# Encoder layer on one core: ten of 22 inner tiles by seven products in the first down stage, and another order of first norm, attention scores and tail

## The chip, the cores and the metric

The kernel runs on one core of a Trainium2 chip. The metric is the device time in microseconds of one execution. The kernel before has a median of 1548.7 us over 3 runs (1548.59 to 1549.08).

## The reference

One step of an encoder layer over 576 tokens (512 of a new stream, 64 of a running one), width 1024, inner width of the FFN 2816, which is 22 tiles of 128:

```
h = LN1(ALPHA * x + 0.5 * swiglu_ffn(x, w_gu, w_down))
z = h @ w_in          # mLSTM q, k, v, o, i, f | attention q, k, v | gates g_m, g_a
h = LN2(ALPHA * h + w_out(sig(g_m) * P_m(mLSTM(h)) + sig(g_a) * P_a(BandAttn(h))))
y = LN3(ALPHA * h + 0.5 * swiglu_ffn(h, w_gu2, w_down2))

swiglu_ffn(x, w_gu, w_down) = (silu(gate) * up) @ w_down     # gate, up = split(x @ w_gu)
```

All in float32, with 4 mLSTM heads of 256 and 16 attention heads of 64, and the new states of both returned.

## The kernel before, in words

**Numbers.** Data lie transposed: a tile is 128 features by 576 tokens, taken as two halves of 288 (slices `A` and `B`). TensorE multiplies in a rounded format. So each operand is split in a rounded high part and the rest, the low part, and a product of a weight tile and a data half is three matmuls: high by high, high weight by low data, low weight by high data (L135 is the helper `mm`). For a weight piece of 128x1024, ScalarE makes the high part `wh` (L149, `act`) and VectorE subtracts to get the low part `wl` (L152, `tt`). Some low parts are made instead by ScalarE and a DMA of POOL that adds the weight from memory (`add_lo`, L195). Takes of results out of PSUM are `stt` (L155) or `tt`.

**Order of the work.** The program is written out in the order of TensorE's matmuls. Everything else is queued with `later(time, function)` and issued as a running count of TensorE time passes by; a scheduler then puts the instructions of each engine in a fixed order by priority (`hot` raises it, `issue_after` ties an instruction behind another). Each engine works through its own list in that order. Weights come through a plan: `pump` (L232) loads the next raw piece with SP into one of 2 buffers `wr`, then splits it into one of `NWB` = 4 pairs `wh`, `wl`; `take` and `done` (L296, L306) mark use and release.

**The first down stage** (`ffn`, L1203; from 256.05 us of the profile to 392.6). The output has 8 tiles of 128. Output tiles 1, 3 and 5 are half made ahead by `plain` (L1132), one matmul triple for each inner tile and token half. For a pair of output tiles (j, j+1) `seven` (L1150) covers eight of the 22 inner tiles: it treats the two outputs, two groups of four inner tiles and the two token halves as a 2x2 by 2x2 product and makes it with seven products instead of eight, on sums of weights and sums of data. Each product is 4 tiles x 3 = 12 matmuls of 288 columns, 84 for the pair. The sums of weights come in four pieces: `a` (the two blocks of output j: a11, a12), `t` (t0, t1), `u` (q1, a22) and `v` (q0). `split_ds` (L209) makes three sums of 128x512 on VectorE into the raw buffers when `t` is due, and a fourth into a buffer of its own for `v`. The products run in the order a11, a12, t0, q1, q0, t1, a22, with takes (`ln.take`) after the first and third to seventh. The remaining 14 inner tiles are `plain` in two pieces of 8 and 6 (`DC`, L375). For j = 6 the two outputs' plain parts run before the seven.

**Hidden tiles.** `Hidden.upto` (L1111) splits the hidden activations into high and low parts `h`, `hb`, `hc` in the order `ORDER`, each tied behind the one before. `Inner.part` (L866) makes the sums of data and their parts.

**First norm** (`Norm`): squares and sums `s1`, `s2` are gathered as output tiles finish (`last`, L599; `moments`, L632); `stats` makes mean and variance with matmuls on columns of ones, POOL takes the power, `spread` and `apply` (L755) multiply by gain and 1/sigma (`stt` with `rb` from PSUM), add the bias on ScalarE and split the result for the first product with `w_in`. For the tiles 0 and 1 this is done at high priority.

**Attention.** `att_qkv(j)` (L1487) prepares head pair group j, `att_core` (L1607) makes its scores: for each block a score matmul, a VectorE pass that adds the bias and takes the minimum (L1627), exp on ScalarE, reciprocal (L1619) and scaling on VectorE or POOL (L159), a transpose on TensorE. Between them run products with `w_in`. `dup` writes keys once more, rounded (`kh`) and rest (`kl`).

**Tail** (`turned`, L701): the third norm's last tile, with columns of sums and a matmul `mb` with the mean, then 8 transposes, four `stt` of 128x512 and four stores.

Of the kernel before, what the change touches and what calls it, by code (L numbers as in the profile page):

```python
# [88 lines left out]
def tile_layer(ctx: ExitStack, tc: tile.TileContext, ins, outs):  # L89
# [92 lines left out]
    HALVED = {("in", c + j) for c in (32, 40) for j in range(3, KT)}  # L182
# [26 lines left out]
    def split_ds(c):  # L209
# [3 lines left out]
        lo = wpool.tile([P, 1024], F32R, tag="wl", name=nm("wl"), bufs=NWB)  # L213
        a, b = slice(0, 512), slice(512, 1024)
# [17 lines left out]
    def pump(limit=None):  # L232
        limit = limit or wst["ahead"]
        while True:
# [9 lines left out]
            if wst["dma"] < min(len(plan), c + 2):  # L244
# [6 lines left out]
                wst["load"] = SP.dma_start(raws[i][:, :src.shape[1]], src)  # L251
# [7 lines left out]
            if c < wst["stop"] and plan[c][0][0][:2] != "ds" and c < wst["taken"] + limit and wst["used"] < NWB:  # L259
# [10 lines left out]
                else:  # L270
                    lo = wpool.tile([P, 1024], F32R, tag="wl", name=nm("wl"), bufs=NWB)
                    step = n if plan[c][0] not in PIECES else 512
                    if plan[c][0] in HALVED:
                        for a in (0, 512):
                            act(hi[:, a:a + 512], raw[:, a:a + 512])
# [99 lines left out]
    DC = ((0, 8), (8, 8), (16, 6))  # L375
# [5 lines left out]
    def plan_ffn(n):  # L381
# [5 lines left out]
        def chunk(j, c):  # L387
            k0, nk = DC[c]
# [123 lines left out]
    class Norm:  # L512
# [86 lines left out]
        def last(self, j, cc, end=None):  # L599
# [3 lines left out]
            act(sq, d, AF.Square)  # L603
            tt(s1, s1, d, ALU.add)
# [96 lines left out]
        def turned(self, hf, dh, sq):  # L701
# [11 lines left out]
            for q, s in ((0, s1), (1, self.hs(self.s2, hf)), (0, dh), (1, sq)):  # L713
# [4 lines left out]
                if q == 0:  # L718
                    mm(mb, ones_d, s, s is s1, s is dh)
# [5 lines left out]
            for q in range(2):  # L725
                for b, a in enumerate(blocks):
# [5 lines left out]
                    stt(y, pts[b, q], rs[:, b:b + 1], self.gb[2 + q], ALU.mult, ALU.add)  # L732
                    SP.dma_start(outs["yt"][b, :, q * 512:(q + 1) * 512], y)
# [21 lines left out]
        def apply(self, j, hf, rb):  # L755
# [8 lines left out]
            early = j < 2 and self.gi == 0  # L764
# [38 lines left out]
    class Combos:  # L803


        def __init__(self, xs, raw, sums, nx=NX):
            self.xs, self.raw, self.n, self.sums, self.nx = xs, raw, 0, sums, nx
            self.own = 4
            self.b = {}
# [5 lines left out]
        def begin(self, i):  # L815
            r1, r2 = self.raw[4 + i], self.raw[i]
# [5 lines left out]
        def add(self, i, begun=False):  # L822
            r1, r2 = self.raw[4 + i], self.raw[i]
# [33 lines left out]
    class Inner(Combos):  # L857


        def __init__(self, xs, raw):  # L860
            super().__init__(xs, raw, {})

        def tile(self):
            return slot(F32R)

        def part(self, i):  # L866
# [4 lines left out]
            for n, (ka, kb) in ((1, ("t2", "t4")), (0, ("t1", "t3"))):  # L871
                t, hi, lo = self.sums.pop(2 * i + n), self.tile(), self.tile()
# [5 lines left out]
        def rest(self):  # L878
            a, b = slice(0, HT_), slice(HT_, T)
            for i in range(4):  # L880
                (h1, l1), (h2, l2) = self.xs.p[12 + i], self.xs.p[8 + i]
# [220 lines left out]
    class Hidden(Act):  # L1102


        ORDER = (*range(KT), *range(2 * KT, FT), *range(12, 2 * KT), *range(KT, 12))

        def __init__(self, raw, pools):
            super().__init__([None] * FT)
            self.raw, self.pools, self.prev, self.n = raw, pools, (None, None), 0

        def upto(self, i):  # L1111
            while self.n <= min(i, FT - 1):
                i_, j = self.n, self.ORDER[self.n]
                pool, tag, n = self.pools[(i_ >= NH0) + (i_ >= NH1) + (i_ >= FT // 2)]
                hi, lo = (pool.tile([P, T], F32R, tag=tag, name=nm(tag), bufs=n) for _ in range(2))

                a, b = self.prev
                with tc.issue_after(a.ins) if i_ else nullcontext():
                    a = ACT.activation(hi, self.raw[j], AF.Copy)
                with tc.issue_after(b.ins) if i_ else nullcontext():  # L1120
                    b = tt(lo, self.raw[j], f(hi), ALU.subtract)
# [10 lines left out]
    def plain(n, ts_, hp, cs=(0, 2)):  # L1132

        for c in cs:
            k0, nk = DC[c]
# [14 lines left out]
    def seven(n, j, inner, ln, Y=None, first=None):  # L1150
# [5 lines left out]
        def product(ps, what, xk, start, end=None):  # L1156
            w_, c0 = at[what]
            for w in "atuv":
                if w_ not in ids and w not in ids:
                    ids[w] = take((f"ds{n}", j, w))  # L1160
            wh, wl = parts[ids[w_]]
            for i in range(4):
                ww = slice(c0 + i * P, c0 + (i + 1) * P)
# [16 lines left out]
        if first is None:  # L1180
# [6 lines left out]
            ln.take(j + 1, A, X, ALU.subtract)  # L1187
            return Y, Z
# [9 lines left out]
        product(Z, "t1", "b22", False, "t")  # L1198
        return Y, Z
# [3 lines left out]
    def ffn(xs, n, gi, raw, final=None, prev=None):  # L1203
        hh = {}
        with tc.tile_pool(name=nm("hr"), bufs=FT, side="right", reuse_waits="tile") as hr, \
# [47 lines left out]
            with wstack, tc.tile_pool(name=nm("st"), bufs=1, side="right", reuse_waits="tile") as un.tp, \  # L1253
                    tc.tile_pool(name=nm("sx"), bufs=1, side="right", reuse_waits="tile") as sx:
                combos.pool = un.pool = sx
                hp_ = Hidden(hh, [(h0, "h0", 2 * NH0), None, None, (hr, "h", FT + 1)])
# [30 lines left out]
            n1, n2 = 2 * (NH1 - NH0), FT - 2 * NH1  # L1287
            with tc.tile_pool(name=nm("h1"), bufs=n1, side="right", reuse_waits="tile") as h1, \
# [8 lines left out]
                inner = Inner(hp_, [hh[k] for k in range(8, 16)])  # L1297
                for i in range(4):
# [18 lines left out]
                od.force(lambda: inner.n == 4)  # L1317
# [31 lines left out]
                if n == 1:  # L1349
# [15 lines left out]
                    ln.last(7, B, False)  # L1365
# [1003 lines left out]
```

## Time and profile before

| what | us |
|---|---|
| median of 3 runs | 1548.7 |
| the profiled execution | 1548.38 |
| its span | 1546.7 |
| TensorE busy (11587 matmuls) | 1533.1 |
| VectorE, ScalarE, POOL busy | 1138.6, 898.0, 229.1 |
| first down stage | 256.05 to 392.29 |
| first matmul with w_in behind the norm | 392.63 |
| first store's issue | 1541.63 |

The profile is of one execution; times within it count from the start of its span. Views name a group by its line, engine and tiles: `mm<-s,wh` writes PSUM tile mm from data s and weight wh; `128x288` is the shape of one operation. A number in brackets behind a row is the idle time ahead of it on that engine, with the operation that ended it.

### The profile page before, as it was taken

The numbers are of one execution on the slowest core, as the hardware profiler recorded it, in microseconds if no ns is written. First come the engines' busy times: TensorE is split into PE (matmuls) and PEld (weight loads), VectorE is DVE, ScalarE is ACT, GpSimd is POOL, SyncE is SP. The second block draws the span as 40 slices with busy tenths as digits, with TensorE's granted clock in tenths as the row PEclk, the third lists the DMA queues.
The fourth block names the chain that finished last, engine by engine and source line by source line (L and its number), as shares of the span: only waits on it lengthen the run. The fifth ranks groups of instructions, "written<-read, shape, count | busy, mean of one in ns | idle before, by whom it ended". The sixth has DMA issues, their size and how long they took to land.

```text
span 1546.7 us, 29517 instructions
## 1 busy us (share of the span) xinstructions
PE 1533.1 (99%) x11587; PEld 1518.9 (98%) x11587; DVE 1138.6 (74%) x2114; ACT 898.0 (58%) x1710; POOL 229.1 (15%) x430
## 2 busy tenths in 40 slices
PE   9999999999999999999999999999999999999998
PEld 9999999999999999999999999999999999999998
DVE  7877778675869866777586766755686877788765
ACT  7545457433865667777854877753466454457333
POOL 1000000000210025655311223202111000001000
PEclk9999999999999999999999999999999999999999
DMA  9322223533664448677534755642665323226334
GB/s 261 109 105 87 98 94 91 140 103 99 195 176 141 150 137 212 161 205 175 124 131 143 185 144 139 163 144 82 195 158 128 110 82 109 83 71 147 120 113 150
DMA packets 80259, 211.15 MB, mean 137 GB/s; under 512 B 9080, under 2 KB 20984, under 8 KB 80120
## 3 DMA queue, kind: packets, MB, share of 16 engines
q1 hardware_dynamic: 65144, 169.15, 33.1%
q0 software_dynamic: 11808, 34.28, 12.8%
q10 hardware_dynamic: 3168, 5.83, 1.2%
q8 instruction: 91, 1.49, 0.4%
q14 instruction: 48, 0.39, 0.1%
HBM read 172.27 MB, written 21.63 MB: 125 GB/s over the span
## 4 chain that ended last, share of the span: by engine, by line
PE 47%; DVE 2%; ACT 2%; issue 2%; POOL 1%; POOLq 0%; DVEq 0%; ACTq 0%
PE mm L135 39%; PE aux L135 8%; PE aux L145 1%; ACT wh L149 0%; DVE U L155 0%; ACT L149 0%; DVE tx L152 0%; DVE s L155 0%; ACT sc L149 0%; ACT s L149 0%; DVE wl L152 0%; POOL kh L159 0%; ACT wh L907 0%; ACT D L149 0%; DVE kwl L155 0%
## 5 line engine op out<-in xcount | busy, mean ns | idle before, releaser
L135 PE MATMUL mm<-s,wh 128*128 128x288 f32 (+2 forms) x3659 | 751.4, 298 | 2.6 <-ACT s L149 1.7
L135 PEld LDWEIGHTS mm<-s,wh 128*128 128x128 f32 x3659 | 587.9, 189 | 6.7 <-ACT s L149 2.2
L135 PE MATMUL mm<-s,wl 128*128 128x288 f32 (+2 forms) x1802 | 532.5, 295 | 0.0
L135 PEld LDWEIGHTS mm<-s,wl 128*128 128x128 f32 x1802 | 339.8, 189 | 0.0
L149 ACT ACTIVATE wh<-wr 128x1024 fp32r<-128x1024 f32 (+2 forms) x143 | 134.3, 948 | 152.0 <-PE mm L135 85.4
L152 DVE TENSOR_TENSOR wl<-wr,wh 128x1024 fp32r<-128x1024 f32 (+2 forms) x93 | 107.9, 1168 | 50.0 <-ACT wh L149 49.9
L135 PE MATMUL mm<-tx,wh 128*128 128x288 f32 x677 | 140.5, 296 | 0.8 <-DVE tx L152 0.8
L135 PEld LDWEIGHTS mm<-tx,wh 128*128 128x128 f32 x677 | 109.2, 188 | 1.3 <-DVE tx L152 1.0
L135 PE MATMUL mm<-tx,wl 128*128 128x288 f32 x350 | 103.2, 295 | 0.0
L152 DVE TENSOR_TENSOR wl<-wt,wh 128x1024 fp32r<-128x1024 f32 x51 | 63.8, 1250 | 53.1 <-ACT wh L907 53.0
L907 ACT ACTIVATE wh<-wt 128x1024 fp32r<-128x1024 f32 x51 | 54.0, 1059 | 79.2 <-DVE wt L152 78.1
L152 DVE TENSOR_TENSOR wl<-wu,wh 128x1024 fp32r<-128x1024 f32 x63 | 77.1, 1223 | 29.3 <-ACT wh L907 29.3
L907 ACT ACTIVATE wh<-wu 128x1024 fp32r<-128x1024 f32 x63 | 66.7, 1058 | 40.9 <-PE mm L135 35.3
L135 PE MATMUL mm<-tx,ah 128*128 128x288 f32 x416 | 85.1, 296 | 0.0
L197 POOL DMA_DIRECT2D s<-s x16 | 13.7, 858 | 468.7 <-DVE hb L152 426.7
L149 ACT ACTIVATE h<-h 128x288 f32<-128x288 f32 x78 | 34.0, 436 | 60.9 <-DVE h L152 60.9
L152 DVE TENSOR_TENSOR wl<-ws,wh 128x1024 fp32r<-128x1024 f32 x51 | 62.2, 1220 | 8.9 <-ACT wh L907 8.8
L135 PEld LDWEIGHTS mm<-tx,ah 128*128 128x128 f32 x416 | 66.3, 188 | 0.5 <-ACT c L149 0.4
L135 PEld LDWEIGHTS mm<-tx,wl 128*128 128x128 f32 x350 | 65.7, 188 | 0.0
L152 DVE TENSOR_TENSOR ws<-wu 128x1024 f32<-128x1024 f32 (+1 forms) x55 | 64.7, 1176 | 0.0
L135 PE MATMUL mm<-h,wh 128*128 128x288 f32 (+2 forms) x304 | 62.6, 296 | 0.0
L135 PE MATMUL mm<-tx,al 128*128 128x288 f32 x208 | 61.1, 294 | 0.0
(406 smaller groups left out, 3492.4 us busy)
## 6 DMA issues: line engine op xcount, KB each, us to landing
wu<-in_w_gu SPq DMA_DIRECT2D x78, 512.0 KB, 4.3
wr<-in_w_in SPq DMA_DIRECT2D x48, 512.0 KB, 4.2
wr<-in_w_dn SPq DMA_DIRECT2D x37, 512.0 KB, 3.7
wl<-in_w_in POOLq DMA_DIRECT2D x36, 512.0 KB, 6.5
wu<-in_w_in SPq DMA_DIRECT2D x24, 512.0 KB, 4.7
wr<-in_w_dn SPq DMA_DIRECT2D x19, 384.0 KB, 3.2
s<-s POOLq DMA_DIRECT2D x16, 288.0 KB, 3.6
wu<-in_w_ap SPq DMA_DIRECT2D x8, 512.0 KB, 4.7
```

What stands on the lines that cost most here:

```text
L135: PE.matmul(out, lhsT, rhs, start=start, stop=stop, **kw)
L145: PE.transpose(out, in_, idn)
L149: return ACT.activation(out, in_, func, **kw)
L152: return (eng or DVE).tensor_tensor(out, a, b, op=op)
L197: return POOL.dma_start(lo, src, accum_op=ALU.add)
L907: self.last = ACT.activation(hi, src, AF.Copy)
```

## The change

1. *First down stage.* `seven` takes ten inner tiles for outputs in four pairs: five by five, so 15 matmuls a product, 105 a pair; `plain` keeps 12 inner tiles (8 and 4). The fifth blocks of both outputs come as one more piece `e`, ahead of `a`, `t`, `u`, `v`: two loads of 128x256 into one raw buffer, four sums of 128x128 on VectorE, then high and low part 128x896. `e` holds one of the four weight buffers until the seven ends. Inner tiles are now (12, 13, 14, 15, 17) with (8, 9, 10, 11, 16); the upper ones are held as 288-wide halves, and 16 is the last that is split. Its fifth sums live in buffers `h5`.
2. *First norm.* The square and sum of output 7's second half are issued 3200 later and behind the sixth centred tile; tiles 0 to 3 of the first token half (0 and 1 of the second) are applied at high priority.
3. *Attention.* The low part of the copied keys is tied behind the core's last score; roundings of past keys behind the scaling on POOL (first core) or the last score. Two pieces of `w_in` are rounded in halves.
4. *Tail.* The `mb` matmuls come behind all column sums, the last row's store in two parts.

```
-    HALVED = {("in", c + j) for c in (32, 40) for j in range(3, KT)}
+    HALVED = {("in", c + j) for c in (32, 40) for j in range(2, KT)}
...
+        if what == "e":
+            w = raws.pop(c)
+            a12, a11, t1, t0, a22, q1, q0 = (w[:, i * P:(i + 1) * P] for i in range(7))
+            tt(q0, a11, q1, ALU.add)
+            tt(q1, a22, q1, ALU.add)
+            tt(t0, q1, a11, ALU.add)
+            tt(t1, t0, a12, ALU.add)
+            act(hi[:, :7 * P], w[:, :7 * P])
+            tt(lo[:, :7 * P], w[:, :7 * P], f(hi[:, :7 * P]), ALU.subtract)
+            parts[c] = (hi, lo)
+            return
...
-    DC = ((0, 8), (8, 8), (16, 6))
+    DC = {1: ((0, 8), None, (18, 4)), 2: ((0, 8), (8, 8), (16, 6))}
+    INNER = {1: ((8, 9, 10, 11, 16), (12, 13, 14, 15, 17)), 2: ((8, 9, 10, 11), (12, 13, 14, 15))}
+    AT5 = {"a12": 0, "a11": 1, "t1": 2, "t0": 3, "a22": 4, "q1": 5, "q0": 6}
...
         def seven(j, order="uv"):
+            if n == 1:
+                plan.append(((f"ds{n}", j, "e"), tuple(ins[f"w_dn{n}"][j + e][:, 16 * P:18 * P] for e in range(2))))
             for e, x in enumerate("at"):
...
-        def last(self, j, cc, end=None):
+        def last(self, j, cc, end=None, behind=None):
...
-                if q == 0:
-                    mm(mb, ones_d, s, s is s1, s is dh)
+            for s in (s1, dh):
+                mm(mb, ones_d, s, s is s1, s is dh)
...
-                    stt(y, pts[b, q], rs[:, b:b + 1], self.gb[2 + q], ALU.mult, ALU.add)
-                    SP.dma_start(outs["yt"][b, :, q * 512:(q + 1) * 512], y)
+                    n = 256 if q and b == nb - 1 else 512
+                    for c in range(0, 512, n):
+                        stt(y[:, c:c + n], pts[b, q][:, c:c + n], rs[:, b:b + 1], self.gb[2 + q][:, c:c + n], ALU.mult, ALU.add)
+                        SP.dma_start(outs["yt"][b, :, q * 512 + c:q * 512 + c + n], y[:, c:c + n])
...
-            early = j < 2 and self.gi == 0
+            early = self.gi == 0 and j < (2 if hf else 4)
...
-            for w in "atuv":
+            for w in "eatuv"[n == 2:]:
...
-            wh, wl = parts[ids[w_]]
-            for i in range(4):
-                ww = slice(c0 + i * P, c0 + (i + 1) * P)
+            for i in range(inner.m):
+                wh, wl = parts[ids[w_ if i < 4 else "e"]]
+                ww = slice(c0 + i * P, c0 + (i + 1) * P) if i < 4 else slice(AT5[what] * P, (AT5[what] + 1) * P)
...
-                    ln.last(7, B, False)
+                    later(3200, lambda: ln.last(7, B, False, ln.centred))
...
-                    tt(l_[r, cc], src[r], f(h_[r, cc]), ALU.subtract)
+                    with tc.issue_after(cores[j - 1]["sample"].ins) if e == 0 else nullcontext():
+                        tt(l_[r, cc], src[r], f(h_[r, cc]), ALU.subtract)
...
-                with tc.issue_after(new[1].ins):
+                with tc.issue_after((cores[0]["scaled"] if j == 1 else new[1]).ins):
...
-            later(6000 + 500 * e, lambda e=e: dup(kp, T, NPAST, e))
+            later(6000 + 500 * e, lambda e=e: when("scaled" if j == 1 else "sample", lambda: dup(kp, T, NPAST, e)))
```

**First place: VectorE in the first seven (outputs 0 and 1).** In the kernel before, from the low part of `u` on: `wl_512` is `u`, `wl_518` is `v`, `s_434` and `s_435` are takes (`s_435` from `mm_514` is that of product 1), `h_510` is the low part of the last hidden tile of product 2.

```order
L152 TENSOR_TENSOR wl_501_3361<-wr_470_3218,wh_500_3360 128x1024
L152 TENSOR_TENSOR wl_512_3434<-wr_473_3224,wh_511_3433 128x1024
L155 SCALAR_TENSOR_TENSOR s_434_3040<-s_434_3040,aux_496_3348 128x288
L155 SCALAR_TENSOR_TENSOR s_434_3040<-s_434_3040,aux_497_3349 128x288
L152 TENSOR_TENSOR wl_518_3478<-h_502_3362,wh_517_3477 128x512
L152 TENSOR_TENSOR h_510_3418<-h_241_1624,h_509_3417 128x576
L155 SCALAR_TENSOR_TENSOR s_435_3042<-s_435_3042,mm_514_3471 128x288
```

The same place in the changed kernel, on VectorE: `wr` rows are sums of `t`, `wl_514` is `t`, `wl_524` is `u`, `wl_527` is `v`, `h_519` is the low part of hidden tile 16, and `s_435` from `mm_520` is the take of product 1 and then of product 3.

```order
L155 SCALAR_TENSOR_TENSOR s_434_3040<-s_434_3040,aux_493_3318 128x288
L152 TENSOR_TENSOR wr_496_3333<-wr_496_3333 128x512
L152 TENSOR_TENSOR wr_473_3225<-wr_496_3333,wr_473_3225 128x512
L155 SCALAR_TENSOR_TENSOR s_435_3042<-s_435_3042,mm_520_3456 128x288
L152 TENSOR_TENSOR wr_473_3225<-wr_473_3225 128x512
L152 TENSOR_TENSOR wl_514_3420<-wr_473_3225,wh_513_3419 128x1024
L152 TENSOR_TENSOR wl_524_3463<-wr_496_3333,wh_523_3462 128x1024
L152 TENSOR_TENSOR wl_527_3500<-h_515_3421,wh_526_3499 128x512
L152 TENSOR_TENSOR h_519_3445<-h_321_2239,h_518_3444 128x576
L155 SCALAR_TENSOR_TENSOR s_435_3042<-s_435_3042,mm_520_3456 128x288
```

The take of product 1 stood behind all of t, u, v and the last hidden part; now it stands ahead of the last sum of t, the low parts of t, u and v, and `h_519`.

**Second place: VectorE in the third seven (outputs 4 and 5).** In the changed kernel `s_536` from `mm_580` is the take of product 1, the `wr` rows are the three sums of `t`, `wl_576` is its low part.

```order
L152 TENSOR_TENSOR s2_431_3035<-s2_431_3035,sq_579_3973 128x288
L155 SCALAR_TENSOR_TENSOR s_536_3596<-s_536_3596,mm_580_3978 128x288
L152 TENSOR_TENSOR wr_572_3886<-wr_572_3886 128x512
L152 TENSOR_TENSOR wr_567_3847<-wr_572_3886,wr_567_3847 128x512
L152 TENSOR_TENSOR wr_567_3847<-wr_567_3847 128x512
L152 TENSOR_TENSOR wl_576_3941<-wr_567_3847,wh_575_3940 128x1024
L152 TENSOR_TENSOR wl_584_3985<-wr_572_3886,wh_583_3984 128x1024
```

All sums of `t` stand behind the take.

**Third place: VectorE behind the statistics of the first norm.** In the changed kernel `s_537` from `mm_623` is the take of the last half tile of the down stage, `wl_652` and `wl_661` are the low parts of the second and third pieces of `w_in` (in halves of 512), `s_657` and `s_659` are low parts of normed tiles.

```order
L152 TENSOR_TENSOR s_657_4588<-s_535_3594,s_656_4587 128x288
L152 TENSOR_TENSOR s_537_3598<-s_537_3598,mm_623_4370 128x288
L152 TENSOR_TENSOR s_659_4603<-s_433_3038,s_658_4602 128x288
L152 TENSOR_TENSOR s1_430_3034<-s1_430_3034,s_537_3598 128x288
L152 TENSOR_TENSOR s2_431_3035<-s2_431_3035,sq_667_4645 128x288
L152 TENSOR_TENSOR wl_652_4564<-wr_644_4530,wh_651_4563 128x512 x2
L152 TENSOR_TENSOR s_537_3598<-s_537_3598,c0_429_3033 128x288
L152 TENSOR_TENSOR s_538_3600<-s_538_3600,c0_429_3033 128x288
L155 SCALAR_TENSOR_TENSOR s_536_3596<-s_536_3596,cols_129,aux_645_4541 128x288
L155 SCALAR_TENSOR_TENSOR s_434_3040<-s_434_3040,cols_129,aux_645_4541 128x288
L152 TENSOR_TENSOR sel_4657<-ident_133 64x4
L152 TENSOR_TENSOR wl_661_4614<-wr_650_4561,wh_660_4613 128x512 x2
```

In the kernel before, the low parts of the first two pieces and of half the third stood ahead of that take; now the second stands behind the take and its sums, and the third behind two more tiles of centring and two of gain.

More of the change, by code (lines that the diff above doesn't have):

```diff
@@ L808, in __init__ @@
             self.own = 4
+            self.m = len(raw) // 2
             self.b = {}
@@ L871, in part @@
             for n, (ka, kb) in ((1, ("t2", "t4")), (0, ("t1", "t3"))):
-                t, hi, lo = self.sums.pop(2 * i + n), self.tile(), self.tile()
+                t = self.sums.pop(2 * i + n)
+                hi, lo = ((slot(F32R) if i < 4 else slot(F32R, self.more, "h5", bufs=4)) for _ in range(2))
                 act(hi, t)
@@ L1102, in tile_layer, with __init__ @@
     class Hidden(Act):
-        ORDER = (*range(KT), *range(2 * KT, FT), *range(12, 2 * KT), *range(KT, 12))
-        def __init__(self, raw, pools):
+        def __init__(self, raw, pools, inner):
             super().__init__([None] * FT)
             self.raw, self.pools, self.prev, self.n = raw, pools, (None, None), 0
+            second, first = inner
+            self.ORDER = (*(k for k in range(FT) if k not in first + second), *first, *second)
+            self.half = first if len(first) > 4 else ()
         def upto(self, i):
@@ L1198, in seven @@
         product(Z, "t1", "b22", False, "t")
+        done(ids["e"])
         return Y, Z
@@ L1605, in att_qkv @@
         return st
+    cores = []
     def att_core(j, st):
+        cores.append(st)
         ap_ = apool[0]
```

75 lines of the change are left out of this document (48 added, 27 removed).

## Prediction

> **What bounds the kernel now.** I read the page first, then the chain of waits, the list of who waited for whom, the windows around the first layer norm, and last the timelines of the places that the change touches.
>
> ```profile
> span 1546.7 us, 29517 instructions
> PE 1533.1 (99%) x11587; PEld 1518.9 (98%) x11587; DVE 1138.6 (74%) x2114; ACT 898.0 (58%) x1710; POOL 229.1 (15%) x430
> 1208.90 189.75 PE mm L135 x1428
> ```
>
> TensorE is busy 1533.1 of 1546.7 us; nothing else comes near. The third row is one stretch of the chain: 1428 matmuls of 288 columns in 189.75 us, or 0.133 us each. So a matmul taken out is worth 0.133 us, and every wait that TensorE is made to keep adds its own length. What TensorE waits for now is little:
>
> ```profile
> PE mm L135 <- ACT s L149: 1.7, 1, 1.7
> PE aux L145 <- POOL sc L159: 1.2, 2, 1.0
> 399.27 0.88 PE L135 MATMUL mm<-s,wh 128*128 128x256 f32 x2 [1.73 <-ACT s L149]
> ```
>
> The columns of the first two are total, times, longest. The largest is one gap of 1.73 us, in the first product with w_in just behind the first norm. It has a tail, seen in the windows (granted clock is the number after POOL's):
>
> ```profile
> core 0: us, PE busy (x) PEld busy (x) DVE busy (x) ACT busy (x) POOL busy (x), PEclk, DMA share, GB/s
> 256.00:300.00 44.00, 44.00 (x335) 44.00 (x334) 33.30 (x55) 26.20 (x39) 5.17 (x6) 1.00 0.53 128
> 300.00:386.00 86.00, 86.00 (x650) 85.70 (x650) 58.62 (x97) 28.52 (x48) 1.02 (x2) 1.00 0.35 108
> 401.40:404.70 3.30, 3.30 (x15) 3.01 (x14) 3.30 (x10) 3.30 (x7) 0.00 (x0) 0.50 0.20 70
> 404.80:480.00 75.20, 75.20 (x563) 75.17 (x563) 58.57 (x93) 51.62 (x92) 10.01 (x14) 1.00 0.62 166
> ```
>
> From 256 to 386, the whole down stage of the first FFN, TensorE never rests. After the gap it ran 15 matmuls in 3.30 us at clock 0.50; at the rate of the last row (75.20/563 = 0.134 us) they take 2.0. One such spell costs 1.3 us.
>
> **The change part by part.** *Fewer matmuls.* A pair of output tiles took 84 matmuls by seven products and twice 84 plain; now it takes 105 and twice 72, three fewer. Four pairs: 12 x 0.133 = **-1.6 us**. Sure, if nothing waits.
>
> *What the seven products wait for.* The durations:
>
> ```profile
> L155 DVE SCALAR_TENSOR_TENSOR c<-c,mm 128x288 f32<-128x288 f32 x10 | 4.5, 447 | 0.0
> L152 DVE TENSOR_TENSOR wr<-wr 128x512 f32<-128x512 f32 x8 | 5.5, 692 | 0.2
> L149 ACT ACTIVATE wh<-wr 128x1024 fp32r<-128x1024 f32 x21 | 22.0, 1058 | 36.2 <-DVE wr L152 16.8 <-PE aux L135 10.0 <-PE mm L135 9.4
> L152 DVE TENSOR_TENSOR wl<-wr,wh 128x1024 fp32r<-128x1024 f32 x21 | 25.5, 1224 | 16.6 <-ACT wh L149 16.6
> L152 DVE TENSOR_TENSOR wl<-h,wh 128x512 fp32r<-128x512 f32 x4 | 2.8, 691 | 0.3
> L149 ACT ACTIVATE wh<-h 128x512 fp32r<-128x512 f32 x4 | 2.5, 632 | 13.1 <-PE mm L135 9.4 <-PE aux L135 3.7
> L152 DVE TENSOR_TENSOR h<-h,h 128x576 fp32r<-128x576 f32 x11 | 8.3, 754 | 0.1
> 289.18 0.85 DVE L155 SCALAR_TENSOR_TENSOR s<-s,aux 128x288 f32<-128x288 f32 x2 [2.18 <-PE aux L135]
> 290.11 0.69 DVE L152 TENSOR_TENSOR wl<-h,wh 128x512 fp32r<-128x512 f32 x1
> 290.83 0.76 DVE L152 TENSOR_TENSOR h<-h,h 128x576 fp32r<-128x576 f32 x1
> ```
>
> The last three rows are VectorE in the first seven of before: two takes, the low part of v, and the low part of the last hidden tile, done at 291.6. TensorE needs that one in the fourth tile of product 2, 21 matmuls after the seven began at 289.4, at 292.2: 0.6 us to spare. Now the order is another (the first place shown with the change). The take of product 1 waits for its 15th matmul; call its end T. Behind it on VectorE stand the last sum of t, the low parts of t, u and v, and only then the low part of hidden tile 16, which TensorE wants as fifth tile of product 2, 13 matmuls or 1.73 us after T. VectorE gets there at T + 0.45 (take) + 0.69 (sum) + 1.06 (ScalarE rounds t) + 1.22 (t) + 1.2 (u) + 0.69 (v) + 0.75 = 6.06, 6.1 with the handoffs. TensorE waits 6.1 - 1.73 = **4.35 us**. Were t, u and v ready all along, it would still be ScalarE's 0.63 for v (v's buffer comes free one tile earlier) + 0.69 + 0.75 = 2.1 behind the fourth tile, less 3 matmuls: the floor is about 1.7.
>
> *Third seven (tiles 4, 5).* All three sums of t stand behind the take of product 1: 0.45 + 3 x 0.69 + 1.06 = 3.6 us after T the rounded t is there, and product 3 wants it after 15 matmuls, at 2.0: 1.65 lost with handoffs; its low part comes 1.25 later, when two matmuls (0.27) have run: 1.0 more. **2.7 us**, floor 0 if the takes came sooner. *Second seven.* The shift of tile 0 (two matmuls on a copy) waits for takes that stand behind the sums of t, whose load waits for the new piece e. I find 0 to 2 us, take **0.5**, since the row of this wait in before shows nothing. *Fourth:* the sums have 72 plain matmuls' time; nothing.
>
> *First norm.* In before:
>
> ```profile
> 386.95 0.46 DVE L152 TENSOR_TENSOR s<-s,sq 128x288 f32<-128x288 f32 x1 [0.85 <-ACT sq L149]
> 387.32 1.93 DVE L152 TENSOR_TENSOR s<-s,c 128x288 f32<-128x288 f32 x5
> 389.17 1.29 DVE L152 TENSOR_TENSOR wl<-wr,wh 128x512 fp32r<-128x512 f32 x2
> 390.74 0.93 DVE L155 SCALAR_TENSOR_TENSOR s<-s,cols,aux 128x288 f32<-128x288 f32 x2
> L149 ACT ACTIVATE s<-s,cols 128x288 f32<-128x288 f32 x5 | 2.4, 524 | 0.0
> 392.63 0.38 PE L135 MATMUL mm<-s,wh 128*128 128x256 f32 x1
> 393.43 0.38 PE L135 MATMUL mm<-s,wh 128*128 128x256 f32 x1 [0.42 <-DVE s L152]
> ```
>
> Back to back, a subtraction costs 0.37 (1.93 for five, the last 0.45), a gain 0.42, a half low part 0.60. Now four tiles of the first half are applied at once instead of two. That removes the 1.73 us wait, but the low parts of w_in pieces fall behind (the third place shown with the change). On before's clock the chain starts at 386.95: sum 0.37, four subtractions 1.48, four gains 1.7, s1 0.37, then low parts of tile and weight 0.37 + 0.60 + 0.37 + 0.60, with ScalarE (two operations of about 0.5 for each of four tiles, and a piece's two of 0.63 between) holding the next one to about 393.4; then the take of the last tile, 0.45, a low part 0.65, s1, s2 0.8 and the second piece's half 0.69: 396.1. TensorE starts w_in at 392.25, runs five matmuls of 256 columns (0.133 x 256/288 = 0.118) and waits from 393.0: 3.1. Three matmuls on, the third piece's low part stands behind 0.60 + 2 x 0.37 + 2 x 0.42 + 0.15 + 0.65 = 3.0, less 0.36: 2.6. In sum 5.7 and 0.25 for a piece's rounding, against 3.0 + 0.4 lost in before (0.2, 0.7, 0.2, 1.9 and 0.4 over the usual spacing) and 0.4 from the earlier start: **+2.2**, from -3.4 (all waits and the slow spell gone) to +3.5.
>
> *The clock.* A wait of 1.73 us was followed by a slow spell. New waits over that: first seven, third seven; the norm has one as before. 2 x 1.3 = **+2.6**, from 0 to 5.2 (two spells for 4.35 us, one for the second seven, a second at the norm).
>
> *Attention.*
>
> ```profile
> 612.98 1.25 DVE L152 TENSOR_TENSOR kl<-s,kh 64x576 fp32r<-64x576 f32 x1
> 614.26 0.48 DVE L1627 CUSTOM_DVE_ANT_0 sc<-aux,G 64x320 f32<-64x320 f32 x1
> 614.90 0.30 PE L145 MATMUL aux<-ident,sc 128*128 128x128 f32 x1 [0.69 <-DVE mx L1627]
> 659.66 1.24 DVE L152 TENSOR_TENSOR kl<-s,kh 64x576 fp32r<-64x576 f32 x1
> 661.48 0.39 PE L135 MATMUL aux<-kh,qs 128*128 128x256 f32 x1 [0.59 <-DVE mx L1627]
> 594.87 0.40 POOL L159 TENSOR_SCALAR kl<-kl 64x256 fp32r<-64x256 f32 x1
> 595.37 0.59 POOL L159 TENSOR_SCALAR sc<-sc,mx 128x384 f32<-128x384 f32 x1
> 596.01 0.33 PE L145 MATMUL aux<-ident,sc 128*128 128x128 f32 x1 [0.96 <-POOL sc L159]
> ```
>
> The first two gaps come of a 1.25 us subtraction ahead of the last score; the change moves it behind, and 1.25 exceeds both gaps, so both go (0.69 + 0.59). At 595.37 the scaling stood behind six roundings of past keys; now it is ahead of them: 0.96 more. What is late next: the keys moved back, which TensorE needs a core later (the same subtraction comes again 46.7 us on). The halved pieces cost ScalarE 0.2 us more each beside 42% idle time. **-2.3**, from -3 to +1 (keys late once by a rounding and a subtraction on POOL).
>
> *Tail.* rsqrt's inputs come first, mean's last:
>
> ```profile
> 1539.36 0.17 ACT L149 ACTIVATE m<-aux 128x2 f32<-128x2 f32 x1
> 1540.12 0.70 POOL L509 TENSOR_TENSOR rs<-var,mhalf 128x2 f32<-128x2 f32 x1 [16.66 <-DVE var L155]
> 1540.85 1.41 DVE L155 SCALAR_TENSOR_TENSOR s<-aux,rs,s 128x512 f32<-128x512 f32 x2 [0.82 <-POOL rs L509]
> ```
>
> The four mean matmuls (256 columns, 0.5 us in all) now follow the sums instead of standing among them, and the two engines take the variance before the mean's two operations; so rs is ready 0.5 to 1 us earlier, but the mean then ends about where rs does now, and the first output row gains little; the split of the last one saves part of a 0.7 us operation and adds a store's issue. **-0.2**, from -0.6 to +0.3.
>
> Sum: -1.6 + 4.35 + 2.7 + 0.5 + 2.2 + 2.6 - 2.3 - 0.2 = +8.25. On the profiled execution (1548.38, span 1546.7 and 1.7 around it) that is 1556.6; the median of the runs, 1548.7, lies 0.3 above. I take **1556.5**.
>
> The skill has a rule here. "TensorE: Matmul & The Clock Gate", Part 1 (The HAM clock gate), of the Trainium skill has the half rate set in after at least one idle window of about 3.4 us, windows running freely. The trace agrees on the length of the spell (clock 0.50 in 401.40 to 404.70) but not on the cause: the 1.73 us wait was enough. By the page alone only the wait of 4.35 us could lower the clock.
>
> **The rivals.**
>
> *A, faster: the waits are not there.* Low parts come in time wherever they stand, as they do in before from 256 to 386, and the norm's gap and its spell go too. Then -1.6 - 3.4 - 1.3 - 2.3 - 0.2: 1539.6. It decides if hidden tile 16's low part ends within 1.73 us of T; the sum above would have to be 4.3 us too long, of 6.1 in an engine that works in order. For it: before has no wait in that stage. 0.14.
>
> *B, the waits come, the clock stays up in the down stage:* 1556.5 - 2.6 = 1553.9. It needs a spell to follow from more than the wait's length. For it: the row of the 1.73 us wait has another of 0.42 us six microseconds ahead. [...] 0.17.
>
> *C, more spells,* all four of 1.3 that I named as the upper end: 1559.1. 0.12.
>
> *D, the norm gains in full* (-3.4 in place of +2.2, spell gone): 1556.5 - 5.6 - 1.3 = 1549.6 to 1551, if ScalarE's waits there are shorter than I sum. 0.10.
>
> *E, gains and losses cancel* within 0.2% (3 us, about what a measurement of this kernel can tell from no change): 0.05. That the reorder in attention does nothing is +2.3 on any of these.
>
> My own case keeps 0.42. **Range 1546.5 to 1561**: it leaves out A and the end of C. Its slower cases alone span 1552 to 1561. Faster: A and part of E, 0.15. Slower by over 0.2% (past 1551.8): own case, B, C and half of D, with what E gives there, 0.76; the rest, 0.09, same.
>
> **What the profile will show.** Right: an idle of about 4 us ahead of a matmul of aux with h and wh near 288.5, released by DVE h; two gaps of 1.6 and 1.0 ahead of mm with s, wh and wl some 50 us on; two gaps of 2.5 to 3 behind the norm, released by DVE wl; clock 0.50 after each; no gaps from mx at the first two cores. Wrong: TensorE without rest from 256 to 380, or the norm's waits shorter than 1 us.

## The result, and the profile after

The changed kernel takes 1565.88 us (median of 4 runs, 1565.38 to 1567.47), the kernel before 1548.67 beside it: a ratio of 1.0111, 95% interval 1.0098 to 1.0123. It is slower, by 17.2 us. The forecast was 1556.5 with a range up to 1561: the sign was right, the size less than half of what came.

The page of the changed kernel:

```profile
span 1563.3 us, 29562 instructions
PE 1538.7 (98%) x11575; PEld 1525.4 (98%) x11575; DVE 1141.8 (73%) x2139; ACT 901.1 (58%) x1722; POOL 228.4 (15%) x432
```

Its list of who waited for whom (total, times, longest, in us), TensorE's first three rows:

```profile
PE aux L135 <- DVE h L152: 6.1, 1, 6.1
PE mm L135 <- ACT wh L149: 5.5, 2, 3.1
PE mm L135 <- DVE wl L152: 2.7, 2, 1.9
```

TensorE has 12 matmuls fewer, as counted, and is yet busy 5.6 us longer: the same matmuls ran slower. The rest of the loss is idle time that before did not have. The waits one by one, from TensorE's timeline: the first three rows are the down stage, the last three stand behind it.

```profile
294.65 0.61 PE L135 MATMUL aux<-h,wh 128*128 128x288 f32 x1 [6.14 <-DVE h L152]
348.97 0.53 PE L135 MATMUL mm<-s,wh 128*128 128x288 f32 x2 [3.10 <-ACT wh L149]
350.23 0.40 PE L135 MATMUL mm<-s,wl 128*128 128x288 f32 x1 [0.73 <-DVE wl L152]
399.90 0.53 PE L135 MATMUL mm<-h,wh 128*128 128x288 f32 x2 [0.55 <-DVE s L152]
409.97 0.38 PE L135 MATMUL mm<-s,wl 128*128 128x256 f32 x1 [1.93 <-DVE wl L152]
412.74 0.79 PE L135 MATMUL mm<-s,wh 128*128 128x256 f32 x2 [2.39 <-ACT wh L149]
```

And the windows of the three stretches in which the granted clock (the number after POOL's) fell, with a full one behind them:

```profile
core 0: us, PE busy (x) PEld busy (x) DVE busy (x) ACT busy (x) POOL busy (x), PEclk, DMA share, GB/s
292.70:299.40 6.70, 4.75 (x20) 4.75 (x21) 2.13 (x4) 0.00 (x0) 0.00 (x0) 0.50 0.61 220
350.70:354.00 3.30, 3.30 (x16) 3.30 (x15) 1.67 (x3) 0.00 (x0) 0.00 (x0) 0.50 0.76 225
412.10:422.30 10.20, 9.56 (x41) 9.04 (x42) 5.71 (x16) 6.27 (x17) 1.00 (x1) 0.50 0.34 135
422.40:500.00 77.60, 77.60 (x581) 77.47 (x580) 59.94 (x96) 53.66 (x95) 9.99 (x14) 1.00 0.62 168
```

At the last row's 0.134 us each, the matmuls in the three slow stretches lost 4.75 - 20 x 0.134 = 2.1, 1.2 and 4.1 us: 7.3, where before lost 1.3 in one.

The same matmul in both kernels, by its start, splits the loss by stage:

| matmul | before | after | later by |
| --- | --- | --- | --- |
| first mean column of the first norm | 382.70 | 396.94 | 14.2 |
| first score of attention | 578.19 | 597.38 | 19.2 |
| last score of attention | 756.96 | 772.93 | 16.0 |
| end of the span | 1546.7 | 1563.3 | 16.6 |

So the down stage costs 14.2: waits of 10.9 (with 0.90 at 319.71, in the second seven) and 3.3 of slow clock, less 1.6 for the matmuls, make 12.6, and I have not followed the other 1.7. The norm and the first products with w_in cost 5.0: waits of 0.55 + 1.93 + 2.39 and 4.1 of slow clock, less the 1.73 + 0.42 + 1.3 that before lost there, make 5.5, which is 0.5 more than the stage shows. Attention gives 3.2 back. The tail and what lies ahead of it add 0.6.

### The profile page after: what moved, and what is told of

The parts are those of the page before. It is cut to its first block, busy times and chain, and to the rows that moved or that the text cites. A ratio compares the mean times of both kernels' runs of the same rounds, so it can differ in the third digit from the quotient of the medians.

```text
span 1563.3 us, 29562 instructions
## 1 busy us (share of the span) xinstructions
PE 1538.7 (98%) x11575; PEld 1525.4 (98%) x11575; DVE 1141.8 (73%) x2139; ACT 901.1 (58%) x1722; POOL 228.4 (15%) x432
## 4 chain that ended last, share of the span: by engine, by line
PE 87%; DVE 5%; ACT 3%; DMA 3%; issue 1%; POOL 1%; ACTq 0%; SPq 0%; DVEq 0%; POOLq 0%
PE mm L135 72%; PE aux L135 14%; PE aux L145 2%; DMA wr<-in_w_dn 1%; ACT wh L149 1%; DVE wl L152 1%; DMA wr<-in_w_in 1%; ACT sc L149 1%; DVE sc L1672 1%; DVE wr L152 0%; DMA G<-in_rbias 0%; DVE s L152 0%; DVE h L152 0%; ACT s L149 0%; DMA s<-s 0%
## 5 line engine op out<-in xcount | busy, mean ns | idle before, releaser
L135 PE MATMUL mm<-h,wh 128*128 128x288 f32 (+2 forms) x352 | 73.6, 298 | 0.5 <-DVE s L152 0.5
L149 ACT ACTIVATE h<-h 128x288 f32<-128x288 f32 (+1 forms) x80 | 35.4, 442 | 61.1 <-DVE h L152 60.9
```

Source lines behind the costliest of these rows:

```text
L135: PE.matmul(out, lhsT, rhs, start=start, stop=stop, **kw)
L149: return ACT.activation(out, in_, func, **kw)
```

## The experiments

Theory: nearly all of the loss is made by the down part, and its waits go back to `e` standing in rings of buffers that before had a place free. Rivals: the norm's waits are made by the norm part's own order; the clock alone makes the surplus; one wait only hides another. All 12 kernels compute the whole reference. Each ratio is to the kernel before in runs beside it.

**The four parts alone.** Each is one numbered item of the change, applied to the kernel before, with nothing of the other three.

> Only the first down stage is changed (ten inner tiles by seven products); norm, attention and tail are those of the kernel before. Theory (the waits inside the sevens are the stage's own): 12 matmuls less (-1.6 us), waits of about 6.1, 0.9 and 3.8 us in the first three sevens and two or three slow spells of the clock (3 us): about 1561, with a gap near 6 us ahead of an aux matmul with h and wh near 288. Rival (the sevens only wait because the other parts have moved VectorE's work): no gap over 1 us before 380, and 1547. Second rival (the late end of the stage also makes the norm's waits): 1565.

Measured: 1566.6 us, ratio 1.0113 (1.0099 to 1.0127). TensorE's waits in it:

```profile
294.73 0.61 PE L135 MATMUL aux<-h,wh 128*128 128x288 f32 x1 [6.59 <-DVE h L152]
349.10 0.85 PE L135 MATMUL mm<-s,wh 128*128 128x288 f32 x2 [3.29 <-ACT wh L149]
350.36 0.61 PE L135 MATMUL mm<-s,wl 128*128 128x288 f32 x1 [0.41 <-DVE wl L152]
412.25 0.50 PE L135 MATMUL mm<-s,wh 128*128 128x256 f32 x2 [3.64 <-ACT wh L149]
```

The down part alone loses all that the whole change loses. It is slower than the 1561 expected, because it makes a wait behind the norm too, although the norm's order is that of before; that is the second rival. SyncE's timeline of before has the three w_in pieces in one group of issues:

```profile
378.80 7.65 SPq L251 DMA_DIRECT2D wr<-in_w_in  x3
```

In the changed kernel the third piece goes out alone (SyncE's timeline, then ScalarE's):

```profile
407.12 0.33 SPq L266 DMA_DIRECT2D wr<-in_w_in  x1
```

```profile
412.06 1.15 ACT L149 ACTIVATE wh<-wr 128x512 fp32r<-128x512 f32 x2 [3.64 <-DMA wr<-in_w_in]
```

In before the third load was issued by 386.45, six microseconds ahead of the product that is first to use w_in. In the changed kernel it is issued about when that product starts (407.28), and ScalarE stands idle 3.64 us until it has landed. (In the down part alone it is issued at 405.96, 1.8 us ahead of the product, and ScalarE idles 2.66 us for it; that TensorE's wait there is 3.64 too is chance.)

The third piece takes the raw buffer of the first. In before ScalarE begins to round the first piece at 382.77, just behind the first mean column; VectorE has its low part at 386.09, and the third load goes out at 386.12. In the changed kernel the rounding begins at 401.86, 4.9 us behind the mean column. The low part, behind four of the norm's gains on VectorE, is done at 407.06, and the load goes out at 407.12. That the rounding is so late I put down to `e`, which keeps one of the four weight pairs to the end of the last seven: before the down piece that it rounds at 395.03 ScalarE stood idle 4.57 us for a matmul, which I read as a pair being given back. That part is argued, not shown. The four gains go with the norm part, the down part alone has two there; with four the load has about 1.6 us less lead over the product.

> Only the first norm's part is changed (square and sum of the last half tile put off, four tiles at high priority). Theory: the waits of the changed kernel behind the norm (1.9 and 2.4 us, and three slow spells in a row) are made by this part alone: 4 to 5 us more than before, 1553 to 1554. Rival (they follow from the late down stage, whose loads for w_in come too late): the 1.7 us wait of before goes and nothing comes for it: 1545 to 1547.

Measured: 1551.41, ratio 1.0016 (1.0007 to 1.0025). TensorE's one long wait, and the window with slow clock:

```profile
397.71 0.58 PE L135 MATMUL mm<-s,wl 128*128 128x256 f32 x1 [3.49 <-DVE wl L152]
```

```profile
396.20:406.30 10.10, 8.59 (x37) 8.30 (x38) 5.92 (x16) 4.25 (x12) 1.24 (x1) 0.50 0.54 203
```

Slightly slower, though by less than the 4 to 5 us expected: the wait of 1.73 us is gone and one of 3.49 stands in its place, with 10 us of slow clock in place of 3.4.

> Only the attention's part is changed. Theory: the gaps of 0.69, 0.59 and 0.96 us and what hangs on them go, 2.5 to 3.5 us: 1545 to 1546. Rival (the moved key roundings come late somewhere): no gain, 1548.5 or more.

Measured: 1546.62, ratio 0.9982 (0.9973 to 0.9991): faster, close to what was expected. In its list of waits the 1.2 us that `sc` had cost is down to 0.2, and the 1.7 at the norm stays as in before:

```profile
PE mm L135 <- ACT s L149: 1.7, 1, 1.7
...
PE aux L145 <- POOL sc L159: 0.2, 1, 0.2
```

> Only the tail is changed. From the traces of the two kernels the last 25 us are 0.3 us longer with it: 1549.0. Rival (as forecast): 0.2 us shorter, 1548.5.

Measured: 1548.65, ratio 1.0002 (0.9993 to 1.0010): no difference that can be measured, so the two expected times can't be told apart. In the changed kernel's tail `rs` starts 15.1 us later than in before, where the end of the span is 16.6 later, so it is early. But the mean's operations now end last, and the matmul that needs them waits 0.57 us (POOL's timeline, then TensorE's):

```profile
1555.21 0.70 POOL L529 TENSOR_TENSOR rs<-var,mhalf 128x2 f32<-128x2 f32 x1 [15.49 <-DVE var L155]
```

```profile
1556.72 0.47 PE L135 MATMUL aux<-s,s 128*128 128x512 f32 x1 [0.57 <-DVE s L152]
```

In medians against 1548.96 the parts are +17.6, +2.5, -2.3 and -0.3, in sum 17.5; the change is +17.2.

**The order behind the first wait.** In the changed kernel the sum for `v` and the parts of hidden tile 16 share a ring of buffers, so tile 16 may only be split once `v` has been read. Here `v`'s sum has a buffer of its own:

```
-            q = ds["q"] = ds["room"]()[:, :512]
+            q = ds["q"] = (ds["pool"].tile([P, 512], F32, tag="wv", name=nm("wv"), bufs=1) if plan[c][0][0] == "ds1" else
+                           ds["room"]())[:, :512]
```

> The changed kernel, with the sum of weights for v in a buffer of its own (128x512) instead of one of the hidden tiles' buffers; nothing else is edited. Theory (hidden tile 16's low part stands behind v's low part because it takes the buffer in which v's sum lay): it moves ahead of t's last sum, the wait of 6.1 us at the fifth tile of product 2 goes; in its place product 3 waits for t's rounded part and low part, 2 to 3 us in all, since t's load still lands at 285.2. 3 to 5 us less than the changed kernel: 1561 to 1563. Rival (VectorE has no time for it earlier): the wait stays, 1566.

Measured: 1561.56, ratio 1.0081 (1.0067 to 1.0094), as expected. The wait of 6.14 is gone and these two are in its place:

```profile
291.19 0.53 PE L135 MATMUL mm<-s,wh 128*128 128x288 f32 x2 [1.56 <-ACT wh L149]
292.45 0.40 PE L135 MATMUL mm<-s,wl 128*128 128x288 f32 x1 [0.73 <-DVE wl L152]
```

So hidden 16's low part came late through a shared buffer, and behind it stood a late `t`. The third seven and the norm kept their waits (3.19 + 0.41, then 1.93 and 3.53).

**The down part mended.** `e` gets a raw buffer of its own, two of its seven blocks go to a hidden tile's buffer, and `v`'s sum takes `e`'s raw buffer. `e`'s rounding and low part are then made in three operations each instead of one. The rest is the changed kernel (the cut below leaves out these operations and the new places of the blocks):

```
-            a12, a11, t1, t0, a22, q1, q0 = (w[:, i * P:(i + 1) * P] for i in range(7))
+            a12, a11, t0, a22, q1 = (w[:, i * P:(i + 1) * P] for i in range(5))
+            x = ds["room"]()
+            t1, q0 = x[:, :P], x[:, P:2 * P]
...
-            q = ds["q"] = ds["room"]()[:, :512]
+            q = ds["q"] = (ds["e"] if plan[c][0][0] == "ds1" else ds["room"]())[:, :512]
...
+                    raws[i] = ds["pool"].tile([P, 640], F32, tag="we", name=nm("we"), bufs=1)
```

> The changed kernel, with piece e loaded into a raw buffer of its own (128x640, later used for v's sum too), so that t's load need not wait for e's low part; two of e's sums lie in a hidden tile's buffer. Theory (two raw buffers for e, a and t make t late): t's load is issued some 8 us sooner, its sums are done ahead of the take of product 1, and the waits of 6.1 and 3.1 + 0.7 us go with their slow spells: 1552 to 1555, what is left being the waits behind the norm. Rival (the four weight pairs, of which e holds one through the seven, set the pace): t is split no sooner, waits of 3 us and more stay in the first and third seven: over 1560.

Measured: 1559.48, ratio 1.0061 (1.0046 to 1.0076). The first sum of `t`, in VectorE's timeline, starts at 280.22, where it started at 285.27 in the changed kernel:

```profile
280.22 0.69 DVE L152 TENSOR_TENSOR we<-wr,wr 128x512 f32<-128x512 f32 x1 [2.71 <-DMA wr<-in_w_dn]
```

The waits of 6.14 and 3.10 are gone. But TensorE waits elsewhere:

```profile
291.47 0.50 PE L135 MATMUL mm<-s,wh 128*128 128x288 f32 x2 [2.10 <-DVE s L155]
298.20 0.40 PE L135 MATMUL mm<-h,wh 128*128 128x288 f32 x1 [2.81 <-DMA h<-s]
350.25 0.53 PE L135 MATMUL mm<-h,wh 128*128 128x288 f32 x2 [1.33 <-DVE s L152]
404.02 0.38 PE L135 MATMUL mm<-s,wl 128*128 128x256 f32 x1 [1.71 <-DVE wl L152]
407.76 0.80 PE L135 MATMUL mm<-s,wh 128*128 128x256 f32 x2 [3.36 <-ACT wh L149]
```

Against the change the ratio falls by 0.005, or 7.7 us; the time expected is missed. With the load early, the takes (`s`) and a DMA into `h` are late next. Since `v`'s sum moves here too, which alone removes the wait of 6.14, this run shows the effect of the raw buffer on the third seven, where the run before kept its waits of 3.19 and 0.41; on the first seven it shows both together.

**The norm's order.** The norm part alone, with the low parts of two w_in pieces ahead of the norm's own operations on VectorE:

```
-                        with tc.issue_after(before.ins) if before is not None else nullcontext():
+                        with tc.issue_after(before.ins) if before is not None else nullcontext(), \
+                                tc.high_priority(offset=3 * HOT) if plan[c][0] in (("in", 40), ("in", 32)) else nullcontext():
```

> The norm's part alone on the kernel before, and the low parts of the second and third piece of w_in at a higher priority on VectorE, so that the second stands ahead of the norm's gains. Theory (the wait of 3.5 us and the three slow spells behind it come of the place of these low parts in VectorE's order): the wait falls under 1 us, 4 to 5 us less than the norm's part alone: 1546 to 1547.5. Rival (ScalarE's eight operations for four tiles set the time): a wait over 2 us stays, 1550 to 1551.5.

Measured: 1550.26, ratio 1.0007 (0.9998 to 1.0016). The time is that of the rival; the 1546 to 1547.5 expected is missed. The wait of 3.49 for `wl` is gone; TensorE waits for the sums instead:

```profile
397.49 2.72 PE L135 MATMUL aux<-onec,s 128*128 128x1 f32 x12 [2.31 <-DVE s L152]
```

So a wait stays in either order, and the order says who bears it. Whether VectorE or ScalarE sets it is not settled: VectorE works nearly without a break up to these sums, but it stands idle 0.61 us for ScalarE just ahead of 396.61, and ScalarE makes the square of the last half tile, which the sums need, only at 396.49, behind the bias and rounding of a tile.

**Mended down part and attention,** the norm and the tail as before:

> The kernel before with the down stage of ten inner tiles in the mended form (e in a raw buffer of its own) and the attention's part; norm and tail as before. Theory (behind the norm the third piece of w_in is late since e holds a weight pair to the end of the last seven): a wait of 3 to 4 us stays there with its slow spells, in place of before's 1.7 us: 1548 to 1551. Rival (that wait, too, came from the late loads of t): it goes back to before's 1.7 us, and 12 matmuls and the attention's 2.5 us are the gain: 1544 to 1545.

Measured: 1558.18, ratio 1.0055 (1.0042 to 1.0067), which misses the expected time. Its two longest waits:

```profile
298.58 0.53 PE L135 MATMUL mm<-h,wh 128*128 128x288 f32 x2 [3.57 <-DVE s L152]
404.69 0.50 PE L135 MATMUL mm<-s,wh 128*128 128x256 f32 x2 [4.42 <-ACT wh L149]
```

The wait behind the norm is there without the norm part, as in the down part alone, and without the late loads of `t`: the rival is refuted. That it comes of `e`'s weight pair, which the mend leaves as it is, fits but is not shown.

**Freeing a weight pair sooner.** The down part alone, with the product of `q0` moved ahead of that of `a22` in the last seven, so that `v`'s pair comes free 15 matmuls sooner:

```
+        product(X, "q0", "t3", False, "v")
         product(R, "a22", "t4", True)
         ln.take(j + 1, A, R, ALU.subtract)
-        product(X, "q0", "t3", False, "v")
```

> The down stage's part alone, as in the first run of these, but in the last seven (outputs 6 and 7) the product with q0 comes ahead of the one with a22, so that v's weight pair is free 15 matmuls (2.0 us) sooner. Theory (the late third piece of w_in behind the norm comes of the pair that e holds: the next plain piece waits for v's pair, its raw buffer for that, w_in's loads for the raw buffer): the wait of 3.6 us behind the norm falls by 1 to 2 us and perhaps a slow spell with it: 1562 to 1565. Rival (VectorE's order behind the norm delays the loads): the wait stays at 3.5 us, 1566.

Measured: 1570.8, ratio 1.0137 (1.0120 to 1.0153). The wait behind the norm falls from 3.64 to 1.55, but others come:

```profile
403.44 0.53 PE L135 MATMUL mm<-h,wh 128*128 128x288 f32 x2 [0.96 <-DVE s L152]
413.25 0.50 PE L135 MATMUL mm<-s,wh 128*128 128x256 f32 x2 [1.55 <-ACT wh L149]
432.11 0.90 PE L135 MATMUL mm<-s,wh 128*128 128x320 f32 x2 [2.40 <-ACT kf L149]
```

The time expected is not met: this is the slowest of all. The wait is shorter, as expected, but only in part by an earlier load. Behind the norm, with the third piece of w_in (times in us of each span):

| run | third load issued | ahead of the first product with w_in by | rounding begins | TensorE's wait for it |
| --- | --- | --- | --- | --- |
| before | 386.12 | 6.5 | 390.09 | none |
| changed kernel | 407.12 | 0.2 | 412.06 | 2.39, behind 1.93 for the second piece |
| down part alone | 405.96 | 1.8 | 411.57 | 3.64 |
| mended down part and attention | 397.61 | 1.8 | 404.00 | 4.42 |
| this run | 408.25 | 2.6 | 412.56 | 1.55 |

In before ScalarE's idle time ahead of that rounding ended with a matmul, in the other rows with the landing of the load. In this run the load goes out 0.8 us sooner relative to the product than in the down part alone, and takes 4.3 us to the rounding instead of 5.6. So the late load is shown as what TensorE waits for there. That `e`'s weight pair makes it late stays argued: no run has a fifth pair.

**The norm part in two.** First only the put-off of the last square and sum (`later(3200, ...)`), then only the four tiles at high priority (`early = self.gi == 0 and j < (2 if hf else 4)`):

> On the kernel before only this of the norm's part: square and sum of the last half tile but one are put off behind the sixth centred tile; two tiles at high priority, as before. Theory (the four tiles at once crowd VectorE; the put-off is harmless): gemm with w_in starts up to 0.4 us sooner, time 1548 to 1549. Rival (the put-off sums crowd it): 1550 to 1551.5 as with the whole part.

> On the kernel before only this of the norm's part: four tiles of the first token half at high priority instead of two. Theory (these crowd VectorE ahead of the low parts of w_in and the column sums): a wait of 2.5 to 3.5 us in the first product with w_in, slow spells after it, 1550.5 to 1552. Rival: the 1.7 us wait goes and nothing comes for it, 1546.

Measured: 1549.89, ratio 1.0005 (0.9996 to 1.0014), and 1549.63, ratio 1.0008 (0.9999 to 1.0017). Neither can be told from no change: the first is above the 1548 to 1549 expected and the second below its 1550.5 to 1552, both by less than 1 us. The second has the shifted wait, the first keeps the one of before, for `s`:

```profile
401.14 1.07 PE L135 MATMUL mm<-s,wh 128*128 128x256 f32 x2 [2.19 <-ACT s L149]
```

```profile
396.81 0.58 PE L135 MATMUL mm<-s,wl 128*128 128x256 f32 x1 [2.09 <-DVE wl L152]
```

So only for both together is a loss clear of the scatter (2.5 us, interval 1.0007 to 1.0025); which of them gives how much is open.

**Attention and tail without the rest:**

> On the kernel before the attention's and the tail's parts only. Theory: the two add up, 2.5 us from the attention and nothing that can be measured from the tail: 1546 to 1546.5, faster than both kernels. Rival (one undoes the other, or the attention's gain was scatter): 1548.5.

Measured: 1546.65 against 1548.44, ratio 0.9987 (0.9978 to 0.9996), 0.15 us above the expected 1546 to 1546.5. This and attention alone are faster than both kernels; the tail adds nothing that shows.

## Why the prediction was wrong

The sign, the places of the long waits and attention's gain were right, and no rival took place: A (no waits) and B (the clock stays up) are refuted by the waits and the three slow windows, D by the norm part's 1.0016, E by the 17.2 us. C priced more spells, but each at 1.3. Three steps failed.

**The first seven: 4.35 forecast, 6.14 measured.** The step that failed is that VectorE takes product 1 at T, its end. The last matmul of product 1 in the changed kernel, from TensorE's timeline, and VectorE's timeline behind it:

```profile
286.49 0.29 PE L135 MATMUL mm<-hc,wl 128*128 128x288 f32 x1
```

```profile
285.27 0.69 DVE L152 TENSOR_TENSOR h<-wr,wr 128x512 f32<-128x512 f32 x1 [2.50 <-DMA wr<-in_w_dn]
...
287.28 0.69 DVE L152 TENSOR_TENSOR wr<-wr 128x512 f32<-128x512 f32 x1
288.00 0.69 DVE L152 TENSOR_TENSOR wr<-wr,wr 128x512 f32<-128x512 f32 x1
288.61 0.45 DVE L155 SCALAR_TENSOR_TENSOR s<-s,mm 128x288 f32<-128x288 f32 x1
288.97 0.68 DVE L152 TENSOR_TENSOR wr<-wr 128x512 f32<-128x512 f32 x1
290.84 2.36 DVE L152 TENSOR_TENSOR wl<-wr,wh 128x1024 fp32r<-128x1024 f32 x2 [1.18 <-ACT wh L149]
293.11 0.69 DVE L152 TENSOR_TENSOR wl<-h,wh 128x512 fp32r<-128x512 f32 x1
293.83 0.76 DVE L152 TENSOR_TENSOR h<-h,h 128x576 fp32r<-128x576 f32 x1
```

From the take at 288.61 to the end at 294.59 it is 5.98 us, and the forecast chain was 6.06: the chain was right. But the take itself was late. `t`'s raw load was not issued until 281.66, because `e` held one of the two raw buffers until its low part was made; VectorE idled 2.50 us for it and came to the take, with two sums ahead of it, about 1.8 us after product 1 had ended. 4.35 + 1.8 is the 6.14. I had named the same load as a risk in the second seven only (0.5 forecast, 0.90 measured). With `v`'s sum in a buffer of its own the 6.14 went, though `t` was as late; with `e` in a raw buffer of its own as well `t`'s first sum came 5 us forward, and the third seven's wait went too.

**The third seven: 2.7 forecast, 3.10 + 0.73 measured.** The mechanism is the one forecast, sums of `t` behind the take, and the size was short by 1.1. The same step failed. Product 1 ended at 343.89, and VectorE took it at 345.27, 1.4 us later: it had idled for the load of `t` (issued at 338.90) and then had other takes and sums in front. Its first sum of `t`, and the take:

```profile
342.46 0.69 DVE L152 TENSOR_TENSOR h<-wr,wr 128x512 f32<-128x512 f32 x1 [2.44 <-DMA wr<-in_w_dn]
...
345.27 0.45 DVE L152 TENSOR_TENSOR s<-s,mm 128x288 f32<-128x288 f32 x1
```

From the take to the rounded `t` it is 3.6 us, as forecast; 1.65 + 1.4 is the 3.10. The low part's wait is 0.73 for 1.0.

**The norm: +2.2 forecast.** Its two waits, forecast 3.1 and 2.6, came as 1.93 and 2.39, together less than forecast; but the second is not VectorE's, as I had put it. ScalarE's row above shows it waiting for the load of the third w_in piece, and the down part alone has that wait with the old order on VectorE. The step that failed is that VectorE's order alone (the third place shown with the change) decides there; I followed `e` through the sevens, and not out of the last one into the next stage. The first wait is VectorE's, as forecast, and shorter than I summed. That the norm's sum still came near (+2.7 for +2.2) is luck. By itself the norm part does what its own sum said in kind: one wait is exchanged for another.

**The clock: +2.6 forecast, about +6 measured.** I priced a spell at the one that before shows, 15 matmuls in 3.30 us. The changed kernel has one of that length, one of twice and one of three times that. "TensorE: Matmul & The Clock Gate", Part 1 (The HAM clock gate), of the Trainium skill has the half rate set in after at least one idle window of about 3.4 us. By that the waits of 1.93 and 2.39, with matmuls between them, should have cost no clock; they cost the longest spell of all. The wait of 6.14 us is long enough for that rule; those of 3.10 and 0.73 us are not, and a spell of 3.3 us followed them too. The measurement decides.

**Right:** 12 matmuls fewer at 0.133 us; attention -2.3, by itself 0.9982 and 3.2 us between first and last score; the tail near nothing. The terms' misses, 1.8 in the first seven, 0.4 in the second, 1.1 in the third and 3.4 of clock, make 6.7 of the 9.4 us between forecast and result. Of the rest 1.7 is what I haven't followed in the down stage. What is left is small and of both signs: the norm's waits 0.5 over (4.87 for 2.15 is +2.7, for +2.2), the tail and what lies ahead of it 0.8, the distance of the profiled execution (1565.38) from the median 0.5, and attention 0.9 the other way (-3.2 for -2.3).

## What to carry to other kernels

Count the buffers before the operations: here a piece that was added to a ring moved later loads and splits, and a load of the next stage came late too, where the diff shows nothing. Twelve matmuls are 1.6 us, and a serial chain of load, sum, rounding and low part that TensorE ends up waiting for costs more than that at its first miss. Where an engine has little slack, a change of its order can hand the wait on to another operation, as at the norm: try each part of a change by itself, and keep those that win alone, here the attention part.

## What the runs showed of the hardware

The slow spells are close to 3.4, 6.8 or 10.2 us, and what one costs is what the matmuls run in it lose (2.1, 1.2 and 4.1 us in the changed kernel), on top of the wait ahead of it. TensorE was busy 9.56 of 10.20 us in the last one of the changed kernel, and its clock did not come back before the end. How long a spell gets does not follow from the length of the wait alone. With only the four tiles at high priority, a wait of 2.09 us is followed by this:

```profile
396.50:406.60 10.10, 9.79 (x42) 9.37 (x42) 5.93 (x16) 4.82 (x13) 2.99 (x4) 0.50 0.47 168
```

In the mended kernel, waits of 2.10 and 2.81 us are followed by full clock:

```profile
291.50:298.00 6.50, 3.89 (x28) 3.66 (x28) 0.88 (x2) 0.00 (x0) 0.00 (x0) 1.00 0.98 284
298.20:304.00 5.80, 5.64 (x40) 5.41 (x41) 3.62 (x8) 1.69 (x2) 0.00 (x0) 1.00 0.26 62
```

In the same run a wait of only 0.55 us at 392.62, behind a dozen matmuls of one column, is followed by 3.4 us at clock 0.51 with 15 matmuls; the changed kernel has the same wait of 0.55 us at 399.90, and the clock stays at 1.00. What tells these cases apart stays open.
